# Neighbourhood attention on one core: scores in three float32r passes over high and low halves of queries and keys, in place of plain float32 products

## The chip, the cores and the metric

The kernel runs on one core of one Trainium2 chip. The core has five engines that run side by side, each with its own queue of instructions: TensorE (PE; its weight loads are listed apart as PEld), VectorE (DVE), ScalarE (ACT), GpSimd (POOL) and SyncE (SP, which issues most of the DMAs). The metric is the device time of one execution in microseconds (us); less is better.

## The reference

One layer of a hybrid transformer block over 1024 latent tokens (16 rows by 64 columns of a grid) and 256 context tokens, width 1024, all float32. What matters here is the attention half of the token mixer: 8 heads of 64, a clamped window of 8 rows by 16 columns around each query, and all 256 context keys in the same softmax.

```python
def row_block(r):
    rs = jnp.clip(r - kh // 2, 0, rows - kh)
    q_r = lax.dynamic_index_in_dim(qg, r, axis=1, keepdims=False).reshape(B, NA_NCB, NA_QB, H, Dh)
    k_b = lax.dynamic_slice_in_dim(kg, rs, kh, axis=1)[:, :, col_idx]
    v_b = lax.dynamic_slice_in_dim(vg, rs, kh, axis=1)[:, :, col_idx]
    s_loc = jnp.einsum('bnqhd,brnkhd->bhnqrk', q_r, k_b).astype(jnp.float32) * scale
    ...
    s_loc = jnp.where(col_mask, s_loc + bias.astype(jnp.float32), -jnp.inf)
    s_ctx = jnp.einsum('bnqhd,bkhd->bhnqk', q_r, k_ctx).astype(jnp.float32) * scale
    s = jnp.concatenate([s_loc.reshape(B, H, NA_NCB, NA_QB, n_loc), s_ctx], axis=-1)
    p = jax.nn.softmax(s, axis=-1).astype(v.dtype)
    ...
```

Around it stand adaptive normalisation, the projections to pool inputs, queries, keys and values, a pooling mixer, the output projection, and an MLP of width 4096 with squared ReLU.

## The kernel before

**Number formats.** Nearly all large products are float32 products made of float32r ones: an operand is split into a high half (a copy that ScalarE writes as float32r, `high_part`) and a low half (the difference, which VectorE writes, `low_part`), and three passes are summed, high x high, high x low, low x high (`three`, lines 197 to 200). The score products of the attention (line 984), the transposes and the value products (line 1060) are plain float32 products.

**Stages.** Start-up and the first projections; context keys (`kcp`, seen as `kc`); the projections of keys and queries as a seven-product scheme (`products`, 24 steps of 12 float32r products each, results `kT[j]` for head pair j with 8 column bands in two halves of 512, and `qT[j][b]` for half b); the attention loop; the output projection; the MLP. In most blocks the order on each engine is written out by hand: `in_order` chains the instructions of the named engines in the order in which the program emits them. That holds for PE, ACT, DVE and SP in the stage of keys and queries and in the attention loop, and for POOL too.

**The attention loop.** There are 32 units: 4 head pairs (j) by 8 column bands of queries (m), 128 queries each. The loop runs over i from 0 to 35 as a software pipeline. In round i unit i gets its scores (`scores`, PE, then line 998 on VectorE, which adds the bias table and the mask and takes the least element), unit i-2 is transposed on PE (`turn`, line 1026) and copied out (line 1040 and half of line 1045 on ScalarE, the other half of 1045 on VectorE), unit i-3 is multiplied with the values (`values`, line 1060), and unit i-4 is scaled (`weighed`, line 1070). The exponentials (line 1007) run on ScalarE. A unit at an edge (m of 0 or 7) has 256 local and 256 context keys, an inner one 384 and 256. The two heads of a pair lie on different 64 partitions, so their products use different halves of the array's rows. Each head's scores take one buffer S of two PSUM banks, and there are two such buffers: a unit's scores can be written when line 998 has read those of the unit before.

**Beside the loop.** Ahead of it come the last query products P7, and in rounds 0 and 1 the products P4 (`last_query`, 12 float32r products each), which finish the second half of the queries of head pairs 0 and 1. In some rounds the output weights are split (`weight_split` in rounds 12, 14, 20, 22 and from 32 on; `mixed_split` in rounds 8, 16, 24, 32), sums of the modulation run on PE (rounds 4, 5, 8), and bias tables are made on POOL (`tables(j + 1)` in round 2 of each head pair, line 883).

**Memory.** `page` takes one of 33 buffers of 128 x 1024; `whl` has 8 buffers of the same size with the tag hl, mostly for weights. A buffer that is taken anew waits for the last reader of what was in it.

Of the kernel before, what the change touches and what calls it, by code (L numbers as in the profile page):

```python
# [11 lines left out]
F32 = mybir.dt.float32  # L12
F32R = mybir.dt.float32r
# [5 lines left out]
P = 128  # L19
# [4 lines left out]
CTX = 256  # L24
# [56 lines left out]
def hybrid_block(ctx, tc, x, ctx_in, w_mod, b_mod, gp1, gp2, w_in, pool_w, rpb, w_out, w1, w2, vectors,  # L81
                 mask, edge, out):
    nc = tc.nc
    sub, mul, add = ALU.subtract, ALU.mult, ALU.add
# [3 lines left out]
    whl = ctx.enter_context(tc.tile_pool(name="whl", bufs=8))  # L88
# [10 lines left out]
    def page(name, dt=F32):  # L99
        return act.tile([P, 1024], dt, tag="pg", name=name)  # L100
# [55 lines left out]
    def split(src, hi, lo, factor=1.0):  # L156
        high_part(src, hi, factor)
        low_part(src, hi, lo, factor)
# [112 lines left out]
    with tc.tile_pool(name="ps1", bufs=6, space=PSUM) as ps1, tc.tile_pool(name="tmp1", bufs=3) as tmp:  # L271
# [614 lines left out]


        kT, qT = [None] * 4, [[None] * 2 for _ in range(4)]
        by_tile = lambda t: t.rearrange("p (m t) -> p m t", t=P)
        query = lambda j, b: by_tile(qT[j][b])[:, :, ::-1]  # L890

# [39 lines left out]
        with in_order(ET.PE, ET.Pool, ET.Activation, ET.DVE, ET.SP) as pooling:  # L931
            banks = {of: [bank(f"p{of}{j}") for j in range(2)] for of in "KQ"}
            use(-1)
            for step, (n, of, j) in enumerate([(n, of, j) for n, of in products for j in range(2)]):
                half_product(n, of, j, banks[of])
                use(step)
                if step in (5, 9, 17):
                    name = {5: "S1", 9: "S4", 17: "S3"}[step]
                    parts = token_operand(name, sraw[name])
                if step in (5, 7, 9, 11, 17, 19):  # L940
                    next(parts)
                    next(parts)
                if step in (7, 11):
                    name = {7: "S4", 11: "S3"}[step]
                    sraw[name] = token_raw(name)
                if step == 14:
                    mask_page()
                if step == 20:
                    tables(0)
                if step in (21, 22):  # L950
                    for g in range(2):
                        pool_mixed(2 * (step - 21) + g)
                kept_product(n, of, j, banks[of][j])


    with (
# [12 lines left out]
        def scores(i):  # L969
            j, m = units[i]  # L970
            inner = 0 < m < NM - 1
            n = NKEY if inner else 4 * P
            o = 1 if m == 0 else 0
            q = qT[j][m // 4]
            cols = slice((m % 4) * P, (m % 4 + 1) * P)
            heads = [slice(e * HD, (e + 1) * HD) for e in range(2)]
            S = [ps_s.tile([P, 1024], F32, tag="S", name=f"S{j}_{m}_{e}") for e in range(2)]
            if inner:
                parts = ((128, kT[j][:, (m - 1) * P : (m + 2) * P]), (512, kc[:, j, :]))
            else:  # L980
                parts = ((0, kc[:, j, :]), (256, kT[j][:, (m + o - 1) * P : (m + o + 1) * P]))
            for c0, keys in parts:
                for e, hs in enumerate(heads):
                    nc.tensor.matmul(S[e][:, c0 : c0 + keys.shape[1]], q[hs, cols], keys[hs], start=True, stop=True)  # L984
            halves = lambda a: a.rearrange("p (a b) -> p a b", a=2)
            for e in range(2):
                t = tabs[j % 2][e]
                sp = att.tile([P, NKEY], F32, tag="sp", name=f"sp{j}_{m}_{e}", bufs=6)[:, :n]
                if inner:
                    s, bt, to = S[e][:, 128:768], t[:, :NKEY], sp  # L990
                else:
                    s, to = halves(S[e][:, 0:512]), halves(sp)
                    if o:
                        bt = halves(t[:, 2 * P : 8 * P])[:, :, P:]
                    else:
                        bt = halves(t[:, NLOC : NLOC + 512])
                nm = sm(f"nm_{i}_{e}", 1, 6)
                nc.vector.tensor_tensor_reduce(out=to, in0=s, in1=bt, scale=1.0, scalar=BIG, op0=add, op1=ALU.min,  # L998
                                               accum_out=nm)
                probs[i, e] = sp  # L1000
                least[i, e] = nm
# [150 lines left out]
        with in_order(ET.PE, ET.Activation, ET.DVE, ET.SP) as projected:  # L1152

            def last_query(n, j):
                half_product(n, "Q", j, last_queries)
                kept_product(n, "Q", j, last_queries[j])

            for j in range(2):
                last_query("P7", j)
            for i in range(N + 4):  # L1160
                if i < N and units[i][1] == 2 and units[i][0] < 3:
                    tables(units[i][0] + 1)
                if i in LOADS:
                    weight_load(0, kks[LOADS.index(i)])
                if i == N:
                    t1 = [out_load(f"to1_{kk}w", kk, 1) for kk in (0, 1)]
                    b22 = [out_load(f"bo22_{kk}w", kk, 1) for kk in (2, 3)]
                    t3 = [out_load(f"to3_{kk}w", kk, 1) for kk in (2, 3)]
                    for to, kk in zip(t1, (0, 1)):
                        add_to(halved(to), out_block(kk, 0))  # L1170
                if i == N - 2:
                    G1 = gate_page("a")
                if i > 3:
                    weighed(i - 4)
                    if i % 8 == 3:
                        j = i // 8 - 1
                        add_to(s1a[j], heads[j][:, 512:])
                        add_to(sa2[j], heads[j][:, 512:])

                rest_of_bank = lambda name: pz[:, 256:]  # L1180
                if i == 0:
                    gain = mod_gain(gp1, att.tile([P, 256], F32, tag="gp", name="gpa"), nc.sync)
                if i == 4:
                    mod_gate("a", accs["a"], gain, rest_of_bank)
                    mod_out("a", accs["a"])
                    accs["sh"] = page("accsh2")
                    nc.sync.dma_start(accs["sh"], kept_row)
                if i == 5:
                    column_sums("sc", accs["sc"], scale2, rest_of_bank)
                if i == 8:  # L1190
                    column_sums("sh", accs["sh"], s2, rest_of_bank)
                if i in (1, 2):
                    with tc.issue_after(pooling[ET.Pool]):
                        for k in (2 * i - 2, 2 * i - 1):
                            add_to(s3[k], s1a[k])
                if i in (5, 6):
                    for k in (2 * i - 10, 2 * i - 9):
                        nc.sync.dma_start(sa2[k], s3[k])
                if 8 < i < N and i % 8 == 7:
                    j = i // 8 - 1  # L1200
                    add_to(heads[j][:, :512], sa2[j])
                low()
                if i > 0 and i % 8 == 0:
                    mixed_split(i // 8 - 1)
                for n, at in enumerate(HALVES):
                    if at == i:
                        weight_split(n)
                if i < N:
                    scores(i)
                else:  # L1210

                    t = i - N
                    if t == 0:
                        x, s1 = [], halves_of("so1_")
                    if t % 2 == 0:
                        xs = ps_s.tile([P, 1024], F32, tag="S", name=f"pox{t}")
                        x += [xs[:, :512], xs[:, 512:]]
                    out_sums(x[t], "A11", wo, t, True)
                    nc.scalar.copy(s1[t], x[t])
                if 1 < i <= N + 1:  # L1220
                    turn(i - 2)
                    fifth_kept(i - 2)
                if i < N:
                    exps(i, 0)
                if 1 < i <= N + 1:
                    turn_kept(i - 2, 0, nc.scalar.copy)
                if i < N:
                    exps(i, 1)
                if 1 < i <= N + 1:
                    turn_kept(i - 2, 1, nc.vector.tensor_copy)  # L1230
                if i < 2:
                    last_query("P4", i)
                if 0 < i <= N:
                    share(i - 1)
                if 2 < i <= N + 2:
                    values(i - 3)
                if i > N:
                    out_operand("S1", i - N - 1, s1a[i - N - 1])
# [752 lines left out]
```

## Time and profile before

| | us |
|---|---|
| median of 3 runs | 1033.1 |
| least and most | 1032.53, 1033.29 |
| span of the profiled execution | 1030.8 |
| PE busy in it | 1017.8 |
| DVE busy | 751.8 |
| ACT busy | 543.7 |
| POOL busy | 110.7 |
| line 984, busy on PE, from 218.8 to 322.3 us | 42.52 |

The span runs from the first to the last instruction of one profiled execution. Busy shares are means over stages with different limits, and matmuls are pipelined with modelled ends, so that a busy PE is not PE at its peak. The chain that ended last is followed back from the last instruction: at each step to what released it, or to the instruction before it on its engine. In an order of time each row has the start in us, the duration in us, the engine, the line, the operation, out<-in by the program's names, shapes and count, and in brackets the idle time before it and what ended it.

### The profile page before, as it was taken

The numbers are of one execution on the slowest core, as the hardware profiler recorded it, in microseconds if no ns is written. First come the engines' busy times: TensorE is split into PE (matmuls) and PEld (weight loads), VectorE is DVE, ScalarE is ACT, GpSimd is POOL, SyncE is SP. The second block draws the span as 40 slices with busy tenths as digits, with TensorE's granted clock in tenths as the row PEclk, the third lists the DMA queues.
The fourth block names the chain that finished last, engine by engine and source line by source line (L and its number), as shares of the span: only waits on it lengthen the run. The fifth ranks groups of instructions, "written<-read, shape, count | busy, mean of one in ns | idle before, by whom it ended". The sixth has DMA issues, their size and how long they took to land.

```text
span 1030.8 us, 15588 instructions
## 1 busy us (share of the span) xinstructions
PE 1017.8 (99%) x5782; PEld 834.2 (81%) x5782; DVE 751.8 (73%) x1187; ACT 543.7 (53%) x941; POOL 110.7 (11%) x168
## 2 busy tenths in 40 slices
PE   8999999999999999999999999999999999999997
PEld 6788888877887888888888888888888888888885
DVE  5588767858996587878998887855766666547576
ACT  7573255328887556776655544555543334334431
POOL 3011200244311311310000000000000000000001
PEclk9999999999999999999999999999999999999999
DMA  9999798632337866795786666637967766555556
GB/s 343 332 255 338 246 265 296 204 86 80 72 95 194 203 180 200 253 237 168 267 269 210 204 210 214 205 122 241 327 220 271 248 226 220 202 180 189 176 182 211
DMA packets 123132, 222.68 MB, mean 216 GB/s; under 512 B 9456, under 2 KB 55152, under 8 KB 123056
## 3 DMA queue, kind: packets, MB, share of 16 engines
q1 hardware_dynamic: 96560, 171.14, 50.4%
q0 software_dynamic: 9360, 19.58, 9.5%
q10 hardware_dynamic: 17136, 30.97, 8.0%
q8 instruction: 45, 0.74, 0.3%
q14 instruction: 31, 0.25, 0.1%
HBM read 168.16 MB, written 52.45 MB: 214 GB/s over the span
## 4 chain that ended last, share of the span: by engine, by line
PE 95%; DMA 2%; ACT 1%; DVE 1%; issue 0%; SPq 0%; DVEq 0%; POOLq 0%; ACTq 0%
PE pu L449 4%; PE S L984 4%; PE pa L1060 3%; PE phv L198 3%; PE phz L198 3%; PE phx L198 3%; PE pyx L198 3%; PE phx L200 3%; PE phv L199 3%; PE phx L199 3%; PE pyx L199 3%; PE pyx L200 3%; PE pyv L199 3%; PE pyv L198 3%; PE pyz L199 3%; PE pyz L198 3%
## 5 line engine op out<-in xcount | busy, mean ns | idle before, releaser
L1007 ACT ACTIVATE sp<-sp,nm 128x640 f32<-128x640 f32 (+1 forms) x64 | 51.4, 803 | 20.0 <-DVE nm L998 19.6
L1577 ACT ACTIVATE c<-c 128x512 f32<-128x512 f32 x48 | 30.3, 632 | 47.0 <-DVE c L1697 28.2
L146 ACT CAST wpS<-S 128x512 fp32r<-128x512 f32 x64 | 38.7, 616 | 26.4 <-PE phv L200 9.2
L198 PE MATMUL phx<-thB,wpA 128*128 128x512 f32 x128 | 50.2, 392 | 0.0
L200 PE MATMUL phx<-thB,wpA 128*128 128x512 f32 x128 | 49.8, 389 | 0.0
L199 PE MATMUL phx<-tlB,wpA 128*128 128x512 f32 x128 | 49.8, 389 | 0.0
L152 DVE TENSOR_TENSOR wpS<-S,wpS 128x512 fp32r<-128x512 f32 x64 | 43.4, 685 | 8.3 <-ACT wpS L146 8.3
L998 DVE CUSTOM_DVE_ANT_0 sp<-S,tab 128x640 f32<-128x640 f32 (+1 forms) x56 | 42.9, 803 | 8.8 <-PE S L984 7.3
L1578 ACT ACTIVATE c<-c 128x512 f32<-128x512 f32 x48 | 30.3, 631 | 15.1 <-DVE sa L1660 12.3
L140 POOL TENSOR_TENSOR ry<-vy,nhalf 128x1 f32<-128x1 f32 x8 | 5.9, 740 | 280.7 <-DVE vy L138 280.7
L198 PEld LDWEIGHTS phx<-thB,wpA 128*128 128x128 f32 x128 | 24.0, 188 | 5.5 <-ACT s L1628 0.5
L984 PE MATMUL S<-kT,q 64*128 64x384 f32 (+1 forms) x128 | 27.9, 495 | 0.3 <-DVE nm L998 0.3
L200 PEld LDWEIGHTS phx<-thB,wpA 128*128 128x128 f32 x128 | 24.0, 188 | 5.0
L199 PEld LDWEIGHTS phx<-tlB,wpA 128*128 128x128 f32 x128 | 24.0, 188 | 4.9
L1060 PE MATMUL pa<-pt,v 128*64 128x128 f32 x352 | 25.9, 279 | 0.6 <-ACT px L1040 0.2
L1045 DVE COPY pt<-T 128x512 f32<-128x512 f32 x32 | 22.0, 686 | 5.5 <-PE T L1026 5.5
L198 PE MATMUL phv<-thT,wpA 128*128 128x512 f32 x64 | 25.1, 392 | 0.0
L198 PE MATMUL phz<-thB,wpS 128*128 128x512 f32 x64 | 25.0, 391 | 0.0
L200 PE MATMUL phv<-thT,wpA 128*128 128x512 f32 x64 | 24.9, 389 | 0.0
L199 PE MATMUL phv<-tlT,wpA 128*128 128x512 f32 x64 | 24.9, 389 | 0.0
L200 PE MATMUL phz<-thB,wpS 128*128 128x512 f32 x64 | 24.9, 389 | 0.0
L199 PE MATMUL phz<-tlB,wpS 128*128 128x512 f32 x64 | 24.9, 389 | 0.0
(1100 smaller groups left out, 3359.7 us busy)
## 6 DMA issues: line engine op xcount, KB each, us to landing
b<-in_w SPq DMA_DIRECT2D x64, 512.0 KB, 4.2
hrS<-hdS SPq DMA_DIRECT2D x32, 512.0 KB, 5.1
hrA<-hdA SPq DMA_DIRECT2D x24, 512.0 KB, 5.5
wm<-in_w_mod SPq DMA_DIRECT2D x16, 512.0 KB, 9.7
wa_0w<-in_w SPq DMA_DIRECT2D x16, 512.0 KB, 5.3
wa_1w<-in_w SPq DMA_DIRECT2D x16, 512.0 KB, 4.5
hdA<-c ACTq DMA_DIRECT2D x32, 256.0 KB, 2.8
hdS<-sa ACTq DMA_DIRECT2D x32, 256.0 KB, 2.7
```

The costliest lines, as they stand in the source:

```text
L146: nc.scalar.copy(hi, src)
L152: nc.vector.tensor_tensor(lo, src, hi.bitcast(F32), sub)
L198: nc.tensor.matmul(ps, ahi, bhi, start=first, stop=False, skip_group_check=more)
L199: nc.tensor.matmul(ps, ahi, blo, start=False, stop=False, skip_group_check=more)
L200: nc.tensor.matmul(ps, alo, bhi, start=False, stop=last, skip_group_check=more)
L449: nc.tensor.matmul(pus[b][j], wk(wgt, k, low, j * P, P), r, start=(k == 0 and n == 0), stop=(k == KT - 1 and n == 2))
L984: nc.tensor.matmul(S[e][:, c0 : c0 + keys.shape[1]], q[hs, cols], keys[hs], start=True, stop=True)
L998: nc.vector.tensor_tensor_reduce(out=to, in0=s, in1=bt, scale=1.0, scalar=BIG, op0=add, op1=ALU.min, accum_out=nm)
L1007: nc.scalar.activation(sp, sp, AF.Exp, bias=least[i, e], scale=-1.0, accum_out=sums[i][:, e : e + 1])
L1060: nc.tensor.matmul(pa[e * HD : (e + 1) * HD, cols], v[:, f : f + HD], turns[i][:, e, c] if c < 4 else fifths[i][:, :, (e + 1) * HD : (e + ...
L1577: nc.scalar.activation(r, src, AF.Relu)
L1578: nc.scalar.activation(r, r, AF.Square)
```

## The change

Keys, queries and context keys are split into high and low halves, and each score product becomes three float32r passes.

The context keys are split after step 10 of the stage of keys and queries into two pages; one key half and one query half of head pair 0 after steps 20 and 22. Between the last query products and the loop come four more halves, in round 2 the second query halves of head pairs 0 and 1, and in rounds 3 to 6 two each of the halves of head pairs 2 and 3. Every split is a copy on ScalarE and a subtraction, on VectorE but in rounds 3 to 6, where it is on POOL. A split half fills one buffer with its high and low parts: of `whl` where `small` is set, else a page. Where the local keys of a unit straddle the two halves (m of 3 and 4), they become two pieces of 128 and 256 columns.

```diff
@@ -886,6 +886,15 @@
         kT, qT = [None] * 4, [[None] * 2 for _ in range(4)]
+        keys, queries, kcs = {}, {}, []
+
+        def parts_of(to, j, b, small=False, engine=None):
+            name = f"{'k' if to is keys else 'q'}P{j}_{b}"
+            src = kT[j][:, b * 512 : (b + 1) * 512] if to is keys else qT[j][b]
+            t = whl.tile([P, 1024], F32R, tag="hl", name=name) if small else page(name, F32R)
+            hi, lo = to[j, b] = t[:, :512], t[:, 512:]
+            nc.scalar.copy(hi, src)
+            (engine or nc.vector).tensor_tensor(lo, src, hi.bitcast(F32), sub)
@@ -951,6 +960,13 @@
                 kept_product(n, of, j, banks[of][j])
+                if step == 10:
+                    kcs += [page(f"kc{n}", F32R) for n in "hl"]
+                    split(kcp, *kcs)
+                if step == 20:
+                    parts_of(keys, 0, 0)
+                if step == 22:
+                    parts_of(queries, 0, 0, True)
@@ -971,17 +987,24 @@
-            q = qT[j][m // 4]
+            q = queries[j, m // 4]
+            ck = [a[:, j * CTX : (j + 1) * CTX] for a in kcs]
...
-            if inner:
-                parts = ((128, kT[j][:, (m - 1) * P : (m + 2) * P]), (512, kc[:, j, :]))
-            else:
-                parts = ((0, kc[:, j, :]), (256, kT[j][:, (m + o - 1) * P : (m + o + 1) * P]))
-            for c0, keys in parts:
-                for e, hs in enumerate(heads):
-                    nc.tensor.matmul(S[e][:, c0 : c0 + keys.shape[1]], q[hs, cols], keys[hs], start=True, stop=True)
+            t0, t1 = (m - 1, m + 2) if inner else (m + o - 1, m + o + 1)
+            at = 128 if inner else 256
+            local = []
+            for b in range(2):
+                b0, b1 = max(t0, 4 * b), min(t1, 4 * b + 4)
+                if b0 < b1:
+                    local.append((at + (b0 - t0) * P, [a[:, (b0 - 4 * b) * P : (b1 - 4 * b) * P] for a in keys[j, b]]))
+            parts = local + [(512, ck)] if inner else [(0, ck)] + local
+            for c0, k in parts:
+                for n_q, n_k in ((0, 0), (0, 1), (1, 0)):
+                    for e, hs in enumerate(heads):
+                        nc.tensor.matmul(S[e][:, c0 : c0 + k[0].shape[1]], q[n_q][hs, cols], k[n_k][hs],
+                                         start=(n_q + n_k == 0), stop=(n_q == 1))
@@ -1157,7 +1180,19 @@
             for j in range(2):
                 last_query("P7", j)
+            parts_of(keys, 0, 1, True)
+            parts_of(queries, 1, 0, True)
+            parts_of(keys, 1, 0, True)
+            parts_of(keys, 1, 1)
+            later = [(to, 2, b, True) for b in range(2) for to in (keys, queries)]
+            later += [(to, 3, b, False) for b in range(2) for to in (keys, queries)]
             for i in range(N + 4):
+                if i == 2:
+                    for j in range(2):
+                        parts_of(queries, j, 1)
+                if 3 <= i < 7:
+                    for _ in range(2):
+                        parts_of(*later.pop(0), nc.gpsimd)
```

## The prediction

> **What bounds the kernel now.** I read the page first (span, busy time, the chain of work that ended last), then busy time by stretches, then the chain and the order of time inside the attention loop.
>
> ```profile
> span 1030.8 us, 15588 instructions
> PE 95%; DMA 2%; ACT 1%; DVE 1%; issue 0%; SPq 0%; DVEq 0%; POOLq 0%; ACTq 0%
> ```
>
> The profiled execution spans 1030.8 us; the median of the runs is 1033.1, so 2.3 us lie around the span, and I add my sum to 1033.1. TensorE carries 95% of the chain. What is saved there counts, as long as nothing else takes its place. The score products (line 984) start at 218.8 us and the first product of the output projection at 322.3: the loop is 103.5 us, 3.2 us a unit.
>
> ```profile
> 180.00:200.00 20.00, 20.00 (x90) 16.57 (x89) 17.42 (x22) 6.36 (x9) 0.00 (x0) 1.00 0.76 256
> ...
> 229.30:247.40 18.10, 18.08 (x272) 13.64 (x272) 15.16 (x46) 15.59 (x40) 4.83 (x9) 1.00 0.50 132
> 250.30:322.30 72.00, 71.59 (x1107) 58.35 (x1103) 64.84 (x193) 63.32 (x168) 21.57 (x36) 1.00 0.44 108
> ```
>
> The columns are the stretch, its length, then busy us (and count) of PE, weight loads, DVE, ACT, POOL, the granted clock (1.00), DMA. The second row holds units 3 to 7, the third units 9 to 31. In the third TensorE is busy 71.59 of 72.0, but VectorE 64.84 and ScalarE 63.32: two engines with 7.2 and 8.7 us of room behind the one that binds.
>
> ```profile
> 314.41 0.50 PE T L1026 x16
> 314.90 1.24 PE pa L1060 x20
> 316.15 1.28 PE S L984 x8
> ```
>
> This is the chain near the end of the loop: transposes of the probabilities 0.50, value products 1.24, score products 1.28, then some small transposes (0.18) and the next unit: 3.20 us, PE alone.
>
> ```profile
> 314.26 0.82 DVE L998 CUSTOM_DVE_ANT_0 sp<-S,tab 128x640 f32<-128x640 f32 x1 [0.49 <-PE S L984]
> ...
> 316.08 0.92 PE L984 MATMUL S<-kT,q 64*128 64x384 f32 x4
> ...
> 316.69 0.28 DVE L1070 TENSOR_TENSOR f<-pa,px 128x128 f32<-128x128 f32 x1
> ...
> 317.26 0.22 PE L1026 MATMUL pa<-ident,rb 64*128 64x64 f32 x1
> ...
> 317.46 0.82 DVE L998 CUSTOM_DVE_ANT_0 sp<-S,tab 128x640 f32<-128x640 f32 x1 [0.48 <-PE S L984]
> ```
>
> The same unit from VectorE's side is 317.46 - 314.26 = 3.20 us too: it works to 316.97 (2.71 us) and then waits 0.48 for the scores. A unit can shrink by 0.48 before VectorE is the bound.
>
> **What the change removes and adds on TensorE.** The rows of line 984 (least, median, most ns):
>
> ```profile
> L984 PE MATMUL S<-kcT,q x128: 376/376/480, 218.8 to 319.6; 64*128 64x256 f32 x128
> ...
> L984 PE MATMUL S<-kT,q x128: 376/482/587, 219.4 to 320.0; 64*128 64x384 f32 x96, 64*128 64x256 f32 x32
> ```
>
> Each float32 product stands there as two instructions (32 units x 2 heads = 64 products, 128 records). 128 columns more cost an instruction 482 - 376 = 106 ns, 0.83 ns a column. An inner unit (640 columns, 2 heads, 2 instructions) would be 2.13 us if the heads went in turn. The unit above took 317.26 - 316.08 = 1.18 from its first score product to the next transposes; less a first weight load of 0.11 (below) that is 1.07, half of 2.13. So the two heads, on different 64 rows of the array, run side by side. An edge unit (512 columns) streams 0.85.
>
> After it, three float32r passes for each head and part. No float32r product of 64 rows is in the trace. The nearest row is the first of the stretches: 90 products, float32r of 128 rows and 512 columns, in 20.0 us, 0.222 us each, 0.434 ns a column. I take that rate with the heads side by side. Inner: 3 x 640 x 0.434 = 0.83, so 0.24 saved. Edge: 3 x 512 x 0.434 = 0.67, 0.19 saved. The other bound is heads in turn, twice as long (a rival below).
>
> ```profile
> 219.89 0.19 PEld L198 LDWEIGHTS pqv<-hx,wQT4h 128*128 128x128 f32 x1 [0.33 <-issue]
> 220.00 0.19 PEld L199 LDWEIGHTS pqv<-hx,wQT4h 128*128 128x128 f32 x1
> ```
>
> Each pass loads the query block anew: 12 loads in an inner unit for 8 now. One load can follow another after 0.11 us. That hides behind a 256-column pass (0.11), not behind one of 128 columns (0.056). Such pieces come up in units 3 and 4 of each head pair, where the local keys straddle the two halves: 3 x (0.11 + 0.11 + 0.11) = 1.0, only 0.07 saved. Per 8 units: 4 x 0.24 + 2 x 0.07 + 2 x 0.19 = 1.48 us; 5.9 us over 32 units is the most that the products can give.
>
> [...]
>
> **What of it reaches the end.** In units 9 to 31 the products could give 1.48 x 23/8 = 4.3 us. Six of these 23 units also carry a split of output weights or mixed tokens (a VectorE subtraction of 0.6 us each, a ScalarE copy of 0.5), and 2.71 + 0.6 = 3.3 is more than PE needs: nothing is gained there. 17/23 of 4.3 is 3.2 us, which I take. Bounds: 4.3 if VectorE's lag is made up between the splits; 0.6 if its room, cut from 7.2 to 2.9 us, doesn't suffice for its waits, and only the three edge units without a split gain 0.19 each, where line 998 is 2 x (0.82 - 0.69) = 0.26 us shorter.
>
> **The splits added.**
>
> ```profile
> 197.92 1.12 ACT L146 CAST S3h<-S3r 128x512 fp32r<-128x512 f32 x2
> ...
> 200.51 1.28 DVE L152 TENSOR_TENSOR S3h<-S3r,S3h 128x512 fp32r<-128x512 f32 x2
> ...
> 254.08 4.94 POOL L883 TENSOR_TENSOR tab<-msk,U 128x128 f32<-128x128 f32 x12
> ```
>
> 16 halves of 512 columns and the context keys of 1024: a copy of 512 costs ScalarE 0.56 in a row, a subtraction VectorE 0.64 (0.60 in a longer row). Three places.
>
> Ahead of the loop: the context keys (1.1 us on ACT, 2 x 0.64 = 1.28 on DVE) after step 10, and one key and one query half after steps 20 and 22.
>
> ```profile
> 191.91 1.28 DVE L223 SCALAR_TENSOR_TENSOR acca<-wma_7w,sx,acca 128x1024 f32<-128x1024 f32 x1 [1.33 <-DMA wma_7w<-in_w_mod]
> ...
> 218.94 0.69 DVE L921 TENSOR_TENSOR q<-q,pqv 128x512 f32<-128x512 f32 x1 [2.03 <-PE pqv L200]
> 219.99 0.69 DVE L998 CUSTOM_DVE_ANT_1 sp<-S,tab 128x512 f32<-128x512 f32 x1 [0.37 <-PE S L984]
> 220.73 0.72 ACT L1007 ACTIVATE sp<-sp,nm 128x512 f32<-128x512 f32 x1 [11.04 <-DVE nm L998]
> ...
> 228.43 0.82 DVE L998 CUSTOM_DVE_ANT_0 sp<-S,tab 128x640 f32<-128x640 f32 x1 [0.25 <-PE S L984]
> ```
>
> I cost these at nothing: VectorE's 1.28 us vanish in its wait of 1.33 for a DMA that ends at 191.9, the others in waits for PE such as the 2.03 ahead of 218.94, and ScalarE has 11 us without work. Without that cover the eviction of step 12 would be 1.28 us late, and it has three steps of 12 x 0.222 = 2.7 us before its bank is needed.
>
> Between the last query products and unit 0: four halves. The copies fall into ScalarE's 11 us. The four subtractions (2.4 us) come after the eviction that ends at 219.63, so the first score pass (line 998) starts at 222.05 for 219.99. Queued behind it are unit 0's exponentials and, through the two S buffers, unit 1's scores; but PE has 12 float32r products (12 x 0.222 = 2.7 us) to do meanwhile, and loses about 0.3.
>
> In the loop: before unit 2 two more subtractions (1.2 us), uncovered: line 998 of unit 2 moves from 228.43 to about 229.65, and unit 3's products wait for it.
>
> ```profile
> 240.51 0.56 ACT L1045 COPY pt<-T 128x512 f32<-128x512 f32 x1
> ...
> 241.94 0.67 PE L1026 MATMUL T<-ident,sp 64*128 64x64 f32 x16
> ```
>
> Units 3 to 6 get two copies each on ScalarE, 1.12 us a unit, 4.5 in all, against 18.1 - 15.59 = 2.5 us of room in that stretch: 2.0 us late, part of it the same delay as VectorE's. Behind each pair wait the small copies (1040), the exponentials and half of the copy 1045. For 1045 the next unit's transposes wait, and its slack is 241.94 - 241.07 = 0.87 us (rows above, rounds 5 and 6). Following the queues unit by unit, unit 8 starts some 1.6 us late; with 72.0 - 63.32 = 8.7 us of room over 23 units ScalarE regains 0.3 to 0.4 a unit, until unit 10 is late by 1.1. I take +1.1; bounds 0.3 (only the first loss) and 1.2 + 2.0 = 3.2.
>
> The eight POOL subtractions of 512 columns are in no row: 0.41 us if as long as one of 128 columns, 1.64 at four times; I take 1.64, 13 us in all. Behind them in POOL's queue stand DMA issues of gates and modulation sums that are read from unit 30 on; the first reader of a subtraction's result is unit 16.
>
> **Pages.** The 10 new pages take the place of the kT, q and context pages that the splits free; I cost this at nothing. If the pool is full, the tables of head pair 1 and their load wait some 1.5 us more, and unit 8, which reads them, starts at 247.4.
>
> **After the loop.**
>
> ```profile
> 338.20 7.63 DMA to_3w<-in_w_out
> ```
>
> The chain leaves PE once, for weight loads that follow PE's product ending at 338.2, so an earlier loop end moves them with it. Sum: -3.2 + 1.1 = -2.1: a span of 1028.7 and a time of 1031.0.
>
> **Rivals.**
>
> *All of it counts.* VectorE makes up the splits: -5.9 + 1.1 = -4.8, 1028.3. For: PE is 71.59 of 72.0 busy. Against: VectorE would be at 96%.
>
> *The neighbours take the place.* Only 0.6 gained and 1.1 lost: 1033.6. For: line 998 needs unit i's scores, and unit i+1's scores need line 998, so neither engine works ahead. Against: the 0.48 us of wait in every plain unit.
>
> *The copies on ScalarE decide, slower.* In units 3 to 6 the copy 1045 comes later than its 0.87 us of slack; from there on each 1.12 us is PE's, and with VectorE near its bound nothing is made up: +3.2 - 0.6 = +2.6, 1035.7. Against: 2.5 us of room in that stretch.
>
> *The passes don't run as float32r, or not side by side.* Heads in turn, or two passes' time for each: inner 1.67 for 1.07, edge 1.33 for 0.85: 24 x 0.60 + 8 x 0.48 + 1.1 = +19, 1052. Against: the float32 products of the same shape, side by side by the rows of line 984.
>
> *Loads in line with their head's products.* Inner 6 x 0.11 + 0.83 = 1.49 for 1.18, units 3 and 4 nine loads, 1.82, edge 1.33 for 0.96: 16 x 0.31 + 8 x 0.64 + 8 x 0.37 + 1.1 = +14, 1047. The 1.18 measured speaks against it. [...]
>
> **How the numbers follow.** Chances: the forecast 0.44, all of it 0.16, the neighbours 0.18, the copies 0.12, heads in turn 0.06, loads in line 0.04. About 0.2% (2.07 us) is what a measurement of this kernel can tell from no change; the forecast lies at that edge, so I give 0.24 of it to faster and 0.20 to same, and of the neighbours 0.15 to same and 0.03 to slower. Faster 0.24 + 0.16 = 0.40, same 0.35, slower 0.25. The range reaches from all of it (1028.3, less 0.3 for its own spread) to the copies (1035.7) and leaves out the last two, 0.10, and tails. The forecast's own range is 1029.8 to 1032.2.
>
> **What would show it.** Score products of a plain unit about 0.95 us from first load to transposes for 1.18 (1.8: heads in turn; 1.5: loads in line); units 28 to 30 at about 2.95 us for 3.20; VectorE's wait for S near 0.2; unit 0's line 998 some 2 us later, unit 8's products 1 to 2 us late, and the first output product about 2 us earlier than 322.3. A loop that starts unit 8 over 3 us late, or plain units still at 3.2, proves the sum wrong.

## The result, and the profile after

The changed kernel takes 1035.71 us (median of 14 runs, 1034.81 to 1041.05) against 1033.1 for the kernel before (14 runs, 1032.53 to 1033.37): 2.6 us slower, ratio 1.0032 with a 95% interval of 1.0022 to 1.0042. Run once more beside other kernels it was 2.8 us slower. The forecast was 2.1 us faster; its range reached up to the 1035.7 of its slower rival.

The page of the changed kernel: its span, and the first line of the chain of work that ended last.

```profile
span 1033.5 us, 15965 instructions
...
PE 90%; ACT 4%; DVE 3%; issue 1%; DMA 1%; SPq 0%; ACTq 0%; DVEq 0%; POOLq 0%
```

TensorE's share of the chain fell from 95% to 90%: ScalarE and VectorE now hold 7% of it (2% before). Busy time by stretches says where. The columns are as in the prediction; the first row holds units 3 to 7, the second units 9 to 31 up to the first output product.

```profile
231.54:252.33 20.79, 18.78 (x303) 15.64 (x303) 16.33 (x45) 19.29 (x48) 15.36 (x19) 0.92 0.37 103
255.51:325.76 70.25, 68.84 (x1232) 61.92 (x1230) 64.84 (x191) 62.67 (x169) 21.49 (x36) 1.00 0.42 104
```

The later units are quicker: 70.25 us for 72.0, with VectorE's work the same 64.84. The early ones are slower: 20.79 for 18.1, with PE idle for 2.0 of it, ScalarE busy 19.29 and a granted clock of 0.92. I use the first score product of each unit as a mark and measure from unit 0, so that the start of a profile doesn't count (unit 0 starts between 218.7 and 219.4 in all profiles). All times in us, worked out from the order of time on PE; the last column is the median over that of the kernel before on the same chip. The starts are those of one profiled execution of each kernel, and the ones of e3, e5 and g2 took 1.0, 1.6 and 1.4 us longer than the median of their kernel.

| kernel | unit 3 | unit 4 | unit 9 | units 9 to 31 | median over before |
|---|---|---|---|---|---|
| before | 10.49 | 14.78 | 31.52 | 68.93 | 0 |
| changed | 12.15 | 18.12 | 36.12 | 67.24 | +2.6 |
| changed, again | 12.20 | 19.22 | 36.88 | 67.33 | +2.8 |
| e1, round 2's splits behind the scores | 10.58 | 16.36 | 34.70 | 67.26 | +0.9 |
| e2, gap filled | 12.49 | 17.57 | 35.62 | 67.16 | +1.5 |
| e3, splits one a round | 12.25 | 19.29 | 36.82 | 68.41 | +3.1 |
| e4, one pass | 11.80 | 18.21 | 35.13 | 63.63 | -1.9 |
| e5, plain products | 12.25 | 18.09 | 38.67 | 69.99 | +6.2 |
| f1, on GpSimd | 10.57 | 14.82 | 31.12 | 75.81 | +6.2 |
| f2, behind the round | 10.58 | 15.15 | 39.85 | 73.02 | +12.2 |
| g1, GpSimd, late | 10.61 | 15.13 | 31.85 | 67.12 | -1.8 |
| g2, ScalarE and GpSimd, late | 10.61 | 15.17 | 34.12 | 68.49 | +0.3 |
| g3, ScalarE and VectorE, late | 10.62 | 15.18 | 37.32 | 76.87 | +13.2 |
| h1, GpSimd, same rounds | 10.89 | 15.36 | 40.81 | 67.36 | +6.9 |

So the ramp up to unit 9 costs 36.12 - 31.52 = 4.60 us, the steady part gives 1.69, the part after unit 31 another 0.77, and this profile reached unit 0 0.56 late: 4.60 - 1.69 - 0.77 + 0.56 = 2.7, the difference of the spans. Where the 0.77 comes from no run shows; the profile of e1, which has the same splits and passes, has 0.1 of it.

What happened in round 2 stands in the order of time of the changed kernel (start, us, engine, line, operation, and in brackets the idle time before it and what ended it):

```profile
225.20 5.85 POOL L883 TENSOR_TENSOR tab<-msk,U 128x128 f32<-128x128 f32 x12 [4.05 <-DMA U<-in_rpb]
...
227.97 0.69 DVE L932 TENSOR_TENSOR q<-pqv,q 128x512 f32<-128x512 f32 x1 [1.46 <-PE pqv L200]
...
228.95 1.80 DVE L897 TENSOR_TENSOR qP<-q,qP 128x512 fp32r<-128x512 f32 x2
229.08 0.27 PE L1049 MATMUL pa<-ident,rb 64*128 64x64 f32 x1
...
230.67 0.81 DVE L1021 CUSTOM_DVE_ANT_0 sp<-S,tab 128x640 f32<-128x640 f32 x1
...
231.54 0.38 PE L1006 MATMUL S<-kP,qP 64*128 64x256 f32 x1 [1.69 <-DVE nm L1021]
```

Two subtractions (line 897) stand ahead of unit 2's pass over its scores (line 1021). They take 1.80 us while GpSimd builds tables (first row); a pair while GpSimd does nothing takes 1.28 (221.30 in the same trace). Unit 3 needs the score banks that this pass frees, so TensorE stands idle for 1.69 us. And that is not the end of it. Busy time of the same trace by stretches, with the granted clock as the last column but two:

```profile
229.90:231.50 1.60, 0.00 (x0) 0.00 (x0) 1.60 (x4) 0.00 (x0) 1.60 (x3) 1.00 0.02 8
231.50:233.50 2.00, 1.59 (x23) 1.39 (x25) 1.64 (x5) 1.98 (x4) 1.26 (x2) 1.00 0.61 104
233.50:236.50 3.00, 2.69 (x37) 2.51 (x35) 2.95 (x7) 3.00 (x10) 2.17 (x2) 0.50 0.64 111
```

Two microseconds after the gap the granted clock is 0.50, for about three microseconds (nearly seven in the second profile of this kernel). Unit 3 to unit 4, 4.29 us before, takes 5.97 (7.02 in the second profile).

### The profile page after: what moved, and what is told of

Read it like the earlier page. It is cut to its first block, busy times and chain, and to the rows that moved or that the text cites. A ratio compares the mean times of both kernels' runs of the same rounds, so it can differ in the third digit from the quotient of the medians.

```text
span 1033.5 us, 15965 instructions
## 1 busy us (share of the span) xinstructions
PE 1015.1 (98%) x5958; PEld 840.6 (81%) x5958; DVE 761.1 (74%) x1196; ACT 552.6 (53%) x958; POOL 122.6 (12%) x176
## 4 chain that ended last, share of the span: by engine, by line
PE 90%; ACT 4%; DVE 3%; issue 1%; DMA 1%; SPq 0%; ACTq 0%; DVEq 0%; POOLq 0%
PE pu L449 4%; PE pyx L198 3%; PE pyv L200 3%; PE pyx L200 3%; PE pyz L200 3%; PE pyv L199 3%; PE pyz L199 3%; PE pyx L199 3%; PE pyz L198 3%; PE pyv L198 3%; PE phz L198 3%; PE phv L198 3%; PE phz L199 3%; PE phv L199 3%; PE phv L200 3%; PE phz L200 3%
## 5 line engine op out<-in xcount | busy, mean ns | idle before, releaser
L1006 PE MATMUL S<-kP,qP 64*128 64x256 f32 (+2 forms) x240 | 25.3, 319 | 2.2 <-DVE nm L1021 2.2
L199 PE MATMUL phv<-tlT,wpS 128*128 128x512 f32 x64 | 24.9, 389 | 0.0
```

The lines of the kernel that those rows point to most:

```text
L199: nc.tensor.matmul(ps, ahi, blo, start=False, stop=False, skip_group_check=more)
L1006: nc.tensor.matmul(S[e][:, c0 : c0 + k[0].shape[1]], q[n_q][hs, cols], k[n_k][hs], start=(n_q + n_k == 0), stop=(n_q == 1))
```

## The experiments

**The gap of round 2.** Kernel e1 issues round 2's two splits behind the round's scores instead of ahead of them:

```
-                if i == 2:
-                    for j in range(2):
-                        parts_of(queries, j, 1)
 ...
                     scores(i)
 ...
+                if i == 2:
+                    for j in range(2):
+                        parts_of(queries, j, 1)
                 if i < N:
                     exps(i, 0)
```

> The two splits of round 2 (query halves of block 1) are issued behind the round's scores instead of ahead of them; same instructions, same round. Theory (a gap and the clock behind it): VectorE takes unit 2's scores at about 229.0 us instead of 230.67, PE's wait of 1.69 us ahead of unit 3 falls under 0.5, the granted clock stays at 1.00 where it was 0.50 from 233.5 to 236.9, and unit 9 comes 2.5 to 3 us earlier: 1032.7 to 1033.2. Rival 1 (VectorE and ScalarE are simply full, the work counts wherever it stands): under 0.7 us earlier, 1035.0 to 1035.7. Rival 2 (the copies of rounds 3 to 6 on ScalarE decide): unit 3 comes earlier but unit 9 does not, 1035.2 to 1035.9.

Measured: 1033.61 us, ratio to the kernel before 1.0007 (0.9999 to 1.0016). That is 1.7 to 1.9 us off the changed kernel's loss, for an edit that removes no instruction. The order of time:

```profile
228.67 0.82 DVE L1021 CUSTOM_DVE_ANT_0 sp<-S,tab 128x640 f32<-128x640 f32 x1
...
229.19 1.15 ACT L896 CAST qP<-q 128x512 fp32r<-128x512 f32 x2
...
229.56 0.38 PE L1006 MATMUL S<-kP,qP 64*128 64x256 f32 x1
...
230.23 0.84 ACT L1030 ACTIVATE sp<-sp,nm 128x640 f32<-128x640 f32 x1
```

Unit 3 starts as early as before (10.58 after unit 0), and the clock stays at 1.00. But unit 4 is still 1.6 us late: the two copies (1.15 us) now stand ahead of unit 2's exponential, which starts at 230.23 where its input is ready at about 229.5. TensorE waits 0.93 us for the exponentials (at 232.54), and unit 9 gains 1.4 instead of 2.5 to 3. The total lies 0.4 us above the theory's range and 1.4 below its rivals': the rival that only the amount of work counts falls, and the size was put too high because the same two splits burden ScalarE too.

The trace of e1 also tells what is left of the loss. From unit 2 to unit 9 it takes 26.20 us, 2.91 more than the kernel before (23.29). TensorE's waits on ScalarE's exponentials and small copies there are 0.93, 0.32, 0.84 and 0.45 us, 2.54 together; one more of 0.46 stands behind VectorE, beside GpSimd's subtractions (last section).

**The clock alone.** Kernel e2 leaves the wait and fills it:

```
+                if i == 3:
+                    for _ in range(12):
+                        nc.tensor.matmul(pz[:, 256:512], kcs[0][:, :P], kcs[0][:, 256:512], start=True, stop=True)
                 if i < N:
                     scores(i)
```

> Twelve products of 256 columns, whose sums nothing reads, are added on PE between round 2's transposes and unit 3's scores, where PE stands idle for 1.69 us. They take 12 x 0.11 = 1.3 us of that idle time and save no other work. Theory (the halved clock from 233.5 to 236.9 is the answer to the idle time and costs 3.4 x 0.5 = 1.7 us): the clock stays at 1.00, unit 3 starts where it did (231.5), unit 4 comes 1.5 to 1.7 us earlier, total 1033.9 to 1034.3. Rival (the clock does not cost, units 3 to 6 wait for VectorE and ScalarE anyway): no change or up to 0.3 us more, 1035.6 to 1036.0.

Measured: 1034.19 us, ratio 1.0014 (1.0005 to 1.0023), 1.1 to 1.3 us better than the changed kernel, for twelve more products. In its trace:

```profile
229.46 1.68 PE L1245 MATMUL pz<-kch 128*128 128x256 f32 x12
```

```profile
233.50:236.50 3.00, 2.24 (x42) 1.52 (x38) 2.97 (x7) 3.00 (x8) 2.49 (x2) 1.00 0.25 45
```

Unit 3 is not earlier, the clock is 1.00 in the stretch where it was 0.50, and unit 3 to unit 4 takes 5.08 us for 5.97. Of the 1.5 to 1.7 us expected 0.9 came by unit 4 (1.9 against the second profile of the changed kernel, with its longer halved stretch): the rest lay beside waits for VectorE and ScalarE, which are busy 2.97 and 3.00 of 3.00 there. All five profiles in which PE idles 1.4 to 1.7 us ahead of unit 3 (the changed kernel twice, e3, e4, e5) have the halved clock within some 2 us of it; e1, e2 and g1, whose longest waits are 0.9, 0.8 and 0.4 us, don't have it. The gaps of the other kernels are more mixed (last section).

**Spreading the splits of rounds 3 to 6.** Kernel e3: `if 3 <= i < 11:` with one split a round for `if 3 <= i < 7:` with two.

> The eight splits of rounds 3 to 6 (two a round) are issued one a round in rounds 3 to 10; the same instructions on the same engines. Theory (the copies cost PE only its waits for the small copies, 1.0 to 1.2 us, in rounds 5 to 7): 0.7 to 1.2 us less, 1034.5 to 1035.0, the halved clock still there. Rival (the copies decide): 2.5 to 3.5 us less, 1032.2 to 1033.2. Rival (every copy of 0.56 us costs the same in any round, ScalarE being full): no change, 1035.4 to 1036.

Measured: 1035.86 us, ratio 1.0029 (1.0018 to 1.0041). No gain: 0.3 to 0.5 us more than the changed kernel, too little to tell from no change. The rival that the copies decide falls. The total is what the last rival said, but the trace doesn't show that a copy costs the same in any round. Units 5 to 7 take 6.65 us, for 7.67 and 7.68 in the two profiles of the changed kernel: that is the 1.0 which the theory saw in the clump. Units 7 to 12, where splits now stand, take 17.39 for 15.52 and 15.24, and 0.89 of that loss is a wait of TensorE (at 264.21) behind a VectorE copy of 1.79 us beside GpSimd's subtractions.

**Fewer passes.** Kernel e4 leaves out the high x low and low x high passes of the scores.

> Leaves out two of the three score passes (high x low and low x high); the splits stay. PE's score products of an inner unit fall from 1.0 to about 0.4 us. If PE still bounds a plain unit, the loop of units 9 to 31 shrinks by some 0.55 x 22 = 12 us and the total is 1021 to 1024. If VectorE and ScalarE are the bound as soon as PE is 0.2 us faster (what the missing half of the predicted gain would mean), a plain unit falls from 3.00 to 2.85 at least 2.75, units 9 to 31 by 3 to 6 us, total 1029 to 1032.

Measured: 1030.85 us, ratio 0.9982 (0.9972 to 0.9992). Units 9 to 31 up to the first output product:

```profile
254.43:320.71 66.28, 59.24 (x1024) 48.06 (x1023) 63.76 (x192) 61.66 (x169) 23.90 (x41) 1.00 0.45 111
```

PE is busy 68.84 - 59.24 = 9.6 us less than in the changed kernel, and the stretch is only 4.0 us shorter: VectorE is busy 63.76 of 66.28. This is what the second expectation said: behind the float32r passes VectorE and ScalarE bound most of the loop, and of a still cheaper score product less than half arrives.

**Splits without passes.** Kernel e5 keeps all splits, and computes each score as one float32 product of the high halves; the low halves are not read.

```
-                for n_q, n_k in ((0, 0), (0, 1), (1, 0)):
 ...
+                    nc.tensor.matmul(S[e][:, c0 : c0 + k[0].shape[1]], q[0][hs, cols].bitcast(F32), k[0][hs].bitcast(F32),
+                                     start=True, stop=True)
```

> All splits stay as in the changed kernel; the scores are one plain float32 product of the high halves in place of three float32r passes (the low halves are computed and not read). Theory (the passes save PE 0.2 us in a plain unit and the splits cost the ramp): units 9 to 31 return to 68.9 us plus 0.5 for the splits in them, the ramp stays 4.5 to 5 us over the kernel before, the total is 1037 to 1038.5. Rival (the passes themselves cost what was lost): it is as the kernel before or faster, 1032 to 1033.5.

Measured: 1038.5 us, ratio 1.0064 (1.005 to 1.0078). With the splits and without the passes the kernel is 6.2 us slower than before, at the upper end of what the theory said. Unit 8 is 33.09 after unit 0, as in the changed kernel (32.94; 28.54 before), so the ramp's loss belongs to the splits. From unit 10 to 31 it takes 65.83 us, the kernel before 65.86, the changed kernel 64.36: there the splits cost nothing that can be seen, and the passes give 1.5. In between, units 8 to 10 take 9.74 us, for 6.05 and 6.06: a VectorE copy takes 3.07 us (last section), and from 256.3 to 259.7 the granted clock is 0.50. So the 3.4 to 3.6 us by which e5 is slower than the changed kernel are not the gain of the passes alone.

**All of it on GpSimd.** In kernel f1 the ten splits of rounds 2 to 6 come one a round in rounds 2 to 11, copy and subtraction both on GpSimd:

```
-            nc.scalar.copy(hi, src)
+            if engine is None:
+                nc.scalar.copy(hi, src)
+            else:
+                engine.tensor_copy(hi, src)
 ...
+            later.insert(0, (queries, 0, 1, False))
+            later.insert(5, (queries, 1, 1, False))
 ...
+                if 2 <= i < 12:
+                    parts_of(*later.pop(0), nc.gpsimd)
```

> The ten splits of rounds 2 to 6 are issued one a round in rounds 2 to 11, in the order in which units need them, copy and subtraction both on GpSimd, so that VectorE and ScalarE carry none of them. Theory (what was lost in rounds 2 to 7 is VectorE's subtractions and ScalarE's copies standing ahead of the round's own work, with the idle time and the halved clock that follow): no idle time of PE over 0.5 us in rounds 2 and 3, clock at 1.00, units 9 to 31 as in the changed kernel (67.2 us); total 1030.5 to 1031.8. Rival (GpSimd's work holds VectorE's copies up, 0.23 to 1.1 us each, and that is what costs): ten times some 0.6 us of it on the path, 1034 to 1036.

Measured: 1038.45 us, ratio 1.0059 (1.0046 to 1.0072). The total lies outside both ranges, but the starts tell the theories apart: unit 9 is 31.12 after unit 0, earlier than in the kernel before. The ramp is cured. The time is lost later, at two places; the first in its order of time:

```profile
258.09 0.69 DVE L1071 COPY pt<-T 128x512 f32<-128x512 f32 x1 [2.29 <-DMA gsh<-accsh]
...
259.48 0.27 PE L1052 MATMUL pa<-ident,rb 64*128 64x64 f32 x1 [2.15 <-DVE f L1096]
```

The copy of the transposed probabilities has no wait on that DMA by its data; it needs a page, and the one that it got was still read by the DMA. With splits up to round 11 the sources (4 pages) and the new pages of head pair 3 (4 pages) live at once, and fewer pages lie idle for the round's own work to take. At the second place the copy waits 2.65 us, until 268.19, for GpSimd's tables, and TensorE 3.23. GpSimd's queue has a part in the first: it issues that DMA at 252.71, behind six steps of splits, where the kernel before issues it at 248.28. No run parts the two causes; g1 below changes both (its DMA is issued at 251.01).

**Behind the round.** Kernel f2 has the same rounds as f1, copy on ScalarE, subtraction on VectorE, issued as the last work of the round.

> The same ten splits, one a round in rounds 2 to 11, copy on ScalarE and subtraction on VectorE, issued behind all other work of the round. Theory (the place in the queue decides, but in a plain round VectorE has 0.3 us of room and ScalarE some 0.35 for a split of 0.6 on each): 0.3 us lost in ten rounds, 3 us, in place of 4.6: 1033.0 to 1034.5, no idle time over 0.5 us in round 3, clock at 1.00. Rival (only the order counts, the work is hidden): 1030.5 to 1031.8. Rival (VectorE and ScalarE are full, order is nothing): 1035.2 to 1036.

Measured: 1044.47 us, ratio 1.0119 (1.0104 to 1.0135): far worse than every expectation. I put this down to pages at first; the next set shows that this was wrong.

**Pages out of the way.** Kernels g1, g2 and g3 issue the ten splits in rounds 2, 4, 5, 6, 7, 9 and 19 to 22, so that head pair 3's new pages are those that the first two head pairs have given back:

```
+            later.insert(0, (queries, 0, 1, False))
+            later.insert(1, (queries, 1, 1, False))
+            AT = (2, 4, 5, 6, 7, 9, 19, 20, 21, 22)
 ...
+                if i in AT:
+                    parts_of(*later.pop(0), nc.gpsimd)
```

g1 does both steps on GpSimd (as above); g2 copies on ScalarE and subtracts on GpSimd, g3 copies on ScalarE and subtracts on VectorE, both behind the round's other work. Kernel h1 changes the engine alone: rounds, places and pages as in the changed kernel, both steps on GpSimd.

> As the run with the ten splits on GpSimd one a round, but in rounds 2, 4, 5, 6, 7, 9 and 19 to 22: the four splits of head pair 3, which take new pages, come only when the pages of units 0 to 15 are free again. Theory (in that run the ramp was cured, unit 11 at 256.0, and its 6 us were lost later to pages that come free late): unit 9 at 250.1, units 9 to 31 in 67.2 us, no wait of the copies pt on a DMA or on tables; total 2.3 to 3.3 us under the kernel before on the same chip, 1029.3 to 1030.5. Rival (GpSimd's splits cost wherever they stand, by holding VectorE's copies up): 1033 to 1037.

> The same rounds, each split behind the round's other work; copy on ScalarE, subtraction on GpSimd. Theory (a copy of 0.56 on ScalarE exceeds its room of 0.35 a round by 0.2, in ten rounds): 2 us over the run with both on GpSimd, 1031.5 to 1032.8. Rival (a copy behind the round's work costs nothing): equal to it within 0.5.

> The same rounds, each split behind the round's other work; copy on ScalarE, subtraction on VectorE. Theory (most of the 12 us that this arrangement lost in rounds 2 to 11 were pages; the rest is 0.3 us a round on VectorE and ScalarE): 3 us over the run with both on GpSimd, 1032.3 to 1033.8. Rival (the work itself costs, pages nothing): 1040 to 1045 as there.

> The changed kernel with its places and pages as they are, rounds 2 to 6; only the engine differs: the copies and subtractions of these ten splits all on GpSimd (before: copies on ScalarE, the first two subtractions on VectorE). Theory (what was lost is the work on VectorE and ScalarE): ramp as in the kernel before within 0.5 us as long as the 25 us of GpSimd's work in rounds 2 to 7 release no page late; total 1029.5 to 1031.5. Rival (pages decide, GpSimd's backlog holds them): 1033 to 1038.

*g1*: 1030.76 us, ratio 0.9980 (0.9972 to 0.9988), 1.8 us faster than the kernel before. Busy time of units 3 to 7 and of units 9 to 31:

```profile
229.60:248.02 18.42, 17.91 (x303) 14.60 (x304) 16.51 (x46) 15.47 (x40) 12.97 (x22) 1.00 0.52 143
250.84:320.97 70.13, 68.99 (x1233) 61.95 (x1231) 65.37 (x193) 62.92 (x169) 33.14 (x51) 1.00 0.44 104
```

The early stretch is 18.42 us (18.1 before, 20.79 in the changed kernel), the later one 70.13. The passes' gain is all there, and the rival that GpSimd's work costs wherever it stands falls in the main. What it does cost here: a VectorE copy lasts 1.34 us (at 233.85) beside a subtraction of GpSimd's, and unit 4 to unit 5 takes 4.30 for 3.77.

*g2*: 1032.86, ratio 1.0005 (0.9997 to 1.0013): 2.1 us over g1 for ten copies of 0.56 us on ScalarE, 0.2 each, as expected. The trace, of an execution 1.4 us above the median, has both causes in it. TensorE's waits on ScalarE from unit 2 to unit 9, behind five copies, are 0.25, 0.39 and 0.25 us, which is again 0.2 a copy. Beside them stands one wait for VectorE, behind three subtractions of GpSimd's in a row (246.99 to 250.74):

```profile
247.62 3.21 DVE L1036 COPY rb<-ri 128x128 f32<-128x128 f32 x1
...
251.09 0.27 PE L1049 MATMUL pa<-ident,rb 64*128 64x64 f32 x1 [1.61 <-DVE f L1093]
```

*g3*: 1045.79, ratio 1.0124 (1.0111 to 1.0137). No page is awaited here; a queue is. The order of time in round 6:

```profile
243.58 0.62 ACT L896 CAST kP<-kT 128x512 fp32r<-128x512 f32 x1
...
244.23 0.69 DVE L897 TENSOR_TENSOR kP<-kT,kP 128x512 fp32r<-128x512 f32 x1 [1.26 <-ACT kP L896]
244.84 0.28 DVE L1093 TENSOR_TENSOR f<-pa,px 128x128 f32<-128x128 f32 x1
...
245.18 0.27 PE L1049 MATMUL pa<-ident,rb 64*128 64x64 f32 x1 [1.36 <-DVE f L1093]
```

The copy is the last thing that ScalarE does in the round. The subtraction waits for it at the head of VectorE's queue, VectorE idles 1.26 us with unit work behind it, and TensorE waits 1.36. f2 has the same wait, 1.13 to 1.26 us at each of the five subtractions between 236 and 256 us; my reading of f2 as a matter of pages falls. TensorE's waits behind f2's subtractions are seven, of 0.74 to 1.86 us, 10.0 together, and after the first two of more than 1.6 us the granted clock is 0.50 for 3.4 us each.

*h1*: 1039.5, ratio 1.0063 (1.005 to 1.0076): the rival is right here.

```profile
250.87 0.69 DVE L1071 COPY pt<-T 128x512 f32<-128x512 f32 x1 [7.07 <-POOL qP L900]
```

Unit 4 starts 15.36 after unit 0, so the early ramp is cured too, but GpSimd's 25 us of work in rounds 2 to 7 (ten splits of 1.9 and 6 of tables) run late, a page of queries stays in use until 250.8, and the copy that is given that page waits 7.07 us.

## Why the prediction was wrong

**The passes** cost what was forecast. The heads run side by side and the weight loads (185 ns each) are hidden, as the trace of before said. Rows of a plain unit after the change:

```profile
316.73 0.79 PE L1006 MATMUL S<-kP,qP 64*128 64x384 f32 x6
...
317.36 0.28 PE L1006 MATMUL S<-kch,qP 64*128 64x256 f32 x2
317.48 0.28 PE L1006 MATMUL S<-kcl,qP 64*128 64x256 f32 x2
317.60 0.28 PE L1006 MATMUL S<-kch,qP 64*128 64x256 f32 x2
317.71 0.24 PE L1049 MATMUL pa<-ident,rb 64*128 64x64 f32 x1
...
317.91 0.82 DVE L1021 CUSTOM_DVE_ANT_0 sp<-S,tab 128x640 f32<-128x640 f32 x1 [0.29 <-PE S L1006]
```

A pass of 256 columns for both heads takes 0.12 us (0.111 forecast). From unit 29's first product (316.73) to the next transposes (317.71) it is 0.98 for the 0.95 forecast, VectorE's wait 0.29 for about 0.2, and the last units take 3.18, 3.02 and 3.00 us (2.95 forecast). No run shows heads in turn (1.8 us was worked out) or loads in line with their head's products (1.5): the rows have 0.98, and the two rivals are out.

**The steady gain**, put at 3.2 (0.6 to 4.3), was 1.69. Twelve of the 22 intervals give 1.79, of some 2.0 that fall to them. The four rounds with a split of weights (12, 14, 20, 22) lose 0.37 where I had nothing gained. The two units behind each change of head pair (9 and 10, 17 and 18, 25 and 26) take 5.95, 5.97 and 5.68 us for 5.93, 6.01 and 5.93: 0.27 instead of 1.4. e4 shows why there is no more to have: with VectorE busy 64 us of any such stretch, less work on PE buys little. So the term was mis-sized by counting a gain in every round without a split.

**Ahead of the loop** the splits cost nothing, as forecast: unit 0 starts within 0.6 us in all profiles, and in the changed kernel's own the 0.56 stand already at 150 us, before the first split.

**The step that failed is the ramp: +1.1 forecast (0.3 to 3.2), 4.60 measured** (5.36 in the second profile). Unit 8 starts 4.40 us late, where the prediction worked out 1.6 and named 3 as the sign that its sum is wrong. By unit the 4.60 are 0.25 up to unit 2, 1.41 from unit 2 to 3, 1.68 from 3 to 4 and 1.27 from 5 to 7. The first part held: unit 0's pass came 2 us late and PE lost 0.3 by unit 2. Three things were missed.

(1) Unit 2's pass was put 1.2 us late by two subtractions of 0.6; they took 1.80, and the pass came 1.7 late after the start's shift. I let unit 3 wait for that, and then counted it as overlapping with ScalarE's delay. The wait cost 1.4 us at once. The views of before could have given this: a pair of mixing subtractions took 1.84 us at 205.94 beside GpSimd's tables, 1.29 at 209.20.

(2) I ran TensorE at full clock throughout; the idle time brought the halved clock, which e2 prices at 1.1 to 1.3 us of the total.

(3) ScalarE's copies were set against its room of a whole stretch. Small copies that stand behind the splits let TensorE wait 0.30, 0.89 and 0.44 us in the ramp, 1.63 together. The longest is in round 5, behind a copy (line 621, of modulation sums) that the prediction's list of what waits left out:

```profile
242.41 0.61 ACT L896 CAST qP<-q 128x512 fp32r<-128x512 f32 x1
...
242.94 0.36 ACT L621 COPY accsc<-pz 128x256 f32<-128x256 f32 x1
...
243.35 0.27 PE L1049 MATMUL pz<-ident,rb 64*128 64x64 f32 x1 [0.89 <-ACT accsc L621]
```

**The slower rival**, copies on ScalarE, gave 1035.7, the time that came. That the number fits is in good part luck, as its mechanism is only part of it: TensorE's waits on ScalarE are 1.63 us of the ramp, spreading the copies (e3) brought nothing, moving two splits behind the scores (e1) brought 1.7 to 1.9 us.

**GpSimd's subtractions and the pages**, both put at nothing, cost PE no wait on a page in the changed kernel; h1 and f1 show how near that was. A subtraction took 1.27 us, between the bounds of 0.41 and 1.64. What GpSimd's work does to VectorE was no term of the sum; it stands in the last section.

**The sum**: -1.69 + 4.60 in place of -3.2 + 1.1, and -0.77 after unit 31 that I had not counted. From unit 2 to unit 9 the changed kernel takes 4.35 us more than the kernel before. By TensorE's waits 1.75 of them belong to unit 2's pass (1.69 + 0.36, for 0.30 before) and 1.63 to ScalarE; the 0.97 that remain fit the 0.89 by which e2, with the clock at 1.00, is quicker from unit 3 to 4. This division is an estimate: a wait removed can lay another bare, as e1 shows. What the 0.77 after unit 31 come from stays open.

## What to carry to other kernels

Preparation that a cheaper product needs is work for the engines beside TensorE: find out which of them has room in the very round, not over a stretch, and look at the one that is at a tenth of its time. The same ten splits made the kernel 13 us slower or 2 us faster by engine and place alone. Put a short piece of work neither ahead of what frees a bank (TensorE waited 1.69 us) nor at the tail of a queue whose next engine waits for it (1.36 in g3), expect that an idle TensorE can cost twice (here the gap of 1.69 us, then 3.4 us at a clock of 0.50), don't queue several GpSimd steps in a row beside a copy on VectorE that TensorE waits for (1.82 us in e5, 1.61 in g2), and ask of every later use of a buffer which allocation gets it next.

## What the hardware showed that I had not expected

**The clock after a short gap.** An idle time of 1.69 us (and 0.36 soon after) was followed by a granted clock of 0.50. In the five profiles with such a gap ahead of unit 3 the halved stretch begins 0.1 to 2.0 us after the gap's end and lasts 3.4 us (two profiles) or 6.8 (three).

The length of the gap alone doesn't decide. In f2 the clock is halved behind gaps of 1.69 and 1.67 us (ending at 237.37 and 247.66) and stays at 1.00 behind 1.86, 1.45 and 1.41 (266.09, 270.57, 275.14); it stays at 1.00 behind 1.61 in g2 (251.09) and 2.11 in g3 (262.30) too. Behind 2.15 and 3.23 in f1 it is halved, and in h1 from about 249.8 on, within the longest gap of all, 7.01. Where a profile has two halved stretches inside the loop they begin 10.24 (f1), 10.24 (f2), 23.89 (e5) and 13.65 us (g3) apart, which is 3, 3, 7 and 4 times 3.41, about the length of one short halved stretch. What else than the length of a gap decides is not shown: no run tested it.

**VectorE's copies beside GpSimd's work.** The changed kernel's copy of the shares, 0.23 us in a quiet round, while GpSimd subtracts:

```profile
235.57 1.27 POOL L897 TENSOR_TENSOR qP<-q,qP 128x512 fp32r<-128x512 f32 x1
```

```profile
235.81 1.11 DVE L1036 COPY rb<-ri 128x128 f32<-128x128 f32 x1
```

It ends when the subtraction does (236.84 and 236.92). In e5 the same copy lasted 3.07 us, until the second of two subtractions in a row was done; it starts 0.47 us ahead of the first, and what held it until then the trace doesn't show:

```profile
251.58 3.07 DVE L1035 COPY rb<-ri 128x128 f32<-128x128 f32 x1
...
252.05 1.28 POOL L897 TENSOR_TENSOR kP<-kT,kP 128x512 fp32r<-128x512 f32 x1
...
253.29 1.25 POOL L897 TENSOR_TENSOR qP<-q,qP 128x512 fp32r<-128x512 f32 x1
...
254.90 0.27 PE L1048 MATMUL pa<-ident,rb 64*128 64x64 f32 x1 [1.82 <-DVE f L1092]
```

TensorE waited 1.82 us behind it (in g2 1.61 behind three subtractions, in e3 0.89, in e1 0.46). VectorE's passes over PSUM (0.81 and 0.69) are not longer in these rounds. These rows give the size: a copy of 0.23 us took 1.11 beside one subtraction of GpSimd's, 3.07 beside two in a row (e5) and 3.21 beside three (g2), and VectorE's own pair of subtractions in round 2 took 1.80 beside GpSimd's tables, for 1.28. By what mechanism is not shown. One subtraction at a time, as in g1, cost the loop at most some 0.5 us (unit 4 to 5).
